# A two-block network on one Trainium2 core: full row tile in the feed-forward, mLSTM gates beside a value block, stabiliser spread by one stacked product

## The chip, the cores and the metric

The kernel runs as one launch on one core of one Trainium2 chip. The metric is the device time of an execution in microseconds (us). Before the change three runs took 2161.81, 2165.63 and 2168.8 us; the median is 2165.63 us.

## The reference: what is computed

A first block (two layers, 1024 channels, 16 + 256 positions) is followed by a second block (two layers, 256 latent and 256 context positions). In each layer of the first block a feed-forward stands before and another after the token mixer, four in all, with 2752 hidden channels:

```python
def swiglu_ffn(x, w13, w2):
    a, u = jnp.split(x @ w13, 2, axis=-1)
    return (jax.nn.silu(a) * u) @ w2
```

The first layer of the second block has two mixers side by side, neighbourhood attention (8 heads of 64) and a bidirectional mLSTM (4 heads of 128). Both read the same projection, whose last 16 columns are the mLSTM's gates: input and forget gate, per head and direction. In the chunked reference a stabiliser m keeps the exponentials in range:

```python
        d_in = jnp.where(lower, bcum[..., :, None] - bcum[..., None, :] + ic[..., None, :], -jnp.inf)
        m_inter = bcum + m_st[..., None]
        m_t = jnp.maximum(m_inter, jnp.max(d_in, axis=-1))
        w = jnp.exp(d_in - m_t[..., None])
```

The second layer's mixer is a latent attention; each layer ends with a convolutional feed-forward. Everything is float32.

## The kernel before, in words

**Products.** Activations lie with channels on partitions. A weight chunk (`chunk`, L130) is loaded by SP's queue into one of 4 raw buffers, ACT rounds it to fp32r (`whi`, L140) and DVE subtracts (`wlo`, L141); there are 5 buffers of each. `mm3` (L145) then makes a product of near float32 precision from three fp32r products: high weights with high and low activations (L147, L148), low weights with high activations (L149). Products in plain float32 are used for statistics, transposes and the attention.

**The feed-forward of the first block** (`ffn1`, L363). 43 column tiles of the gate/up product are swept; the first ten come from `raw_tiles`, in which the layer norm is applied to the product instead of the input, with POOL's help. `glu` turns a pair of tiles into a hidden tile and splits it into a tile of 128 partitions x 2 x 272. 2752 channels are 21 tiles of 128 and one of 64; that last one (c == 42) uses `ps[:64]` and `ps[64:128]` of one column tile, fills 64 partitions only, and is the 22nd and last hidden tile. The down-projection (from L398) makes 8 channel tiles; for each it goes over three weight chunks of 8, 8 and 6 row tiles, and over 22 row tiles in all; the last one uses 64 rows of weights and hidden tile (`hw`). DVE adds the residual (L408), ACT and DVE prepare the next norm, POOL sums. Beside the first block's feed-forwards `ada` (L331) computes the modulation vectors of the second block as DVE reductions.

**The first mixer of the second block** (`even`, L1221). `tiles` (L200) makes column tiles over 512 positions; its first `lead` tiles share a sweep over the inputs, first for the context half, then for the latent half, which becomes ready later, after the first block's last norm (PE's statistics `ps_x` and `ps_r`). The lead group here is the four query tiles and a tile with the 16 gate columns spread over 128 (`ev_wg`: forward input at 0, forward forget at 64, backward input at 32, backward forget at 96); the four key tiles follow one by one. `token_tiles` (L1232) makes products with tokens on partitions, two blocks of 256 columns by four token tiles, 24 products of 256 columns each; the attention's values are its first use. `ml_gates` (L1107) makes log forget gates, running sums and running maxima of the gates on ACT and DVE; `ml_cols` (L1138) transposes two of its results to columns. Then the attention runs, with the other mixer's products as filler. In `ml_weights` (L1156), per head, the stabiliser's row for a direction is spread over 128 partitions by a float32 product with a broadcast column of the identity (L1181); DVE masks it (L1183), ACT exponentiates pieces (L1195), DVE multiplies with the scores (L1196). Then two token products (`ps_tt`) serve as filler, and `ml_out` (L1203) applies the weights (`ps_mn`).

**Order.** Each engine runs its queue in order. The order in a queue is made when the program is built: instructions are taken by readiness and by the order in which the code gives them, with a few explicit priorities, and tiles get buffers in the same pass.

Of the kernel before, what the change touches and what calls it, by code (L numbers as in the profile page):

```python
# [11 lines left out]
F32 = mybir.dt.float32  # L12
F32R = mybir.dt.float32r
# [75 lines left out]
class Ker:  # L89
# [61 lines left out]
    def gemm(self, items, X, cols, mark=0, tail=0):  # L151
        """items: (PSUM tile, weight chunk) pairs that share the sweep over the rows of X, but for the last `tail` rows."""
        n = len(X)

        def step(ps, w, k):
            xh, xl = X[k]
            self.mm3(ps, w[0][:, k], w[1][:, k], xh[:, cols], xl[:, cols], k == 0, k == n - 1)

        for k in range(n - tail):
            if k == mark:  # L160
                self.mark = self.last
            for ps, w in items:
                step(ps, w, k)
        for ps, w in items:
            for k in range(n - tail, n):
                step(ps, w, k)

    def raw_tiles(self, srcs, ln, lead=2):
        """As tiles, of a layer norm's output, from its input scaled by the gain alone.

        Yields SBUF tiles that lack only the channel's bias, and the bias; the norm itself is made on the way."""
# [28 lines left out]
    def tiles(self, srcs, X, cols, kt=KD, lead=4, segs=None, hold=()):  # L200
        """Yields PSUM tiles of X @ w, one per 128-column chunk; the first `lead` share a sweep over X,
        one for each of segs, column ranges that become ready one after the other."""
        n = cols.stop - cols.start
        i = 0
        while i < len(srcs):
            g = lead if i == 0 else 1
            items = [((self.mm_ps if j < 4 else self.aux_ps)("ps_g")[:, :n],
                      self.chunk(s, kt, after=hold if 0 < i < lead + 2 else ()))
                     for j, s in enumerate(srcs[i:i + g])]
            if i == 0 and segs:  # L210
                for sl in segs:
                    part = [(ps[:, sl], w) for ps, w in items]
                    for a in ((part,) if sl is segs[0] else (part[:2], *([p] for p in part[2:]))):
                        self.gemm(a, X, sl)
            else:
                self.gemm(items, X, cols, tail=5 if g > 2 else 0)
            for ps, _ in items:
                yield ps
            i += g
# [6 lines left out]
    def mean_b(self, group, d, n, name, ps=None):  # L226
        """Mean over the channels of a group of tiles, the same in each partition."""
# [12 lines left out]
    def sqrt_table(self, after=None):  # L240
        """Have the square root's table in place before the chain that needs it."""
# [6 lines left out]
    def acc(self, S, key, m, src, n, eng):  # L248
        """Running sum over channel tiles; the eighth stays apart for the matmul that ends it."""
# [31 lines left out]
    def ln_raw(self, S, i, m, z, n):  # L281
        """Split of z times the gain of layer norm i, for raw_tiles."""
# [11 lines left out]
    def ln_start(self, S, i, eps, n, off, X):  # L294
        """Mean and reciprocal deviation, the same in each partition."""
# [5 lines left out]
    def ln_apply(self, S, i, eps, n, off, X, M, R, c):  # L301
        """State tile c <- its layer norm i; X gets the split of it."""
# [42 lines left out]
    def ada_cols(self, l):  # L345
        """Per-channel factors of layer l, [128, 8, 2] with the last axis (x, ctx)."""
# [16 lines left out]
    def ffn1(self, l, f, X, raw, n, off, ln):  # L363
        """SwiGLU; state <- 2 alpha state + ffn(state), and the sums of it."""
# [5 lines left out]
        def glu(pa, pu, hw):  # L370
# [5 lines left out]
            else:  # L376
                self.act = nc.scalar.activation(sa[:hw], pa, AF.Silu)
                self.dve = nc.vector.tensor_tensor(out=hr[:hw], in0=pu, in1=sa[:hw], op=ALU.mult)
            self.split(hr[:hw], ht[:hw, 0, :n], ht[:hw, 1, :n])
            hid.append((ht[:hw, 0, :n], ht[:hw, 1, :n]))  # L380
# [17 lines left out]
        for m in range(KD):  # L398
            ps = self.mm_ps("ps_y")[:, :n]
            for q in range(3):  # L400
                kt = 8 if q < 2 else 6
                wh, wl = self.chunk(self.A["w2"][i, m, q][:, :kt * 128], kt)
                for j in range(kt):
                    k = q * 8 + j
                    hw = 64 if k == KF1 - 1 else 128
                    self.mm3(ps, wh[:hw, j], wl[:hw, j], *hid[k], k == 0, k == KF1 - 1)
# [13 lines left out]
    def rope_ret(self, ps, dst):  # L420
        """dst <- ps * cos + halves swapped * signed sin, channels on partitions."""
# [11 lines left out]
    def conv_tap(self, l, u, y, t, j):  # L433
        """One tap of the causal depthwise convolution."""
# [65 lines left out]
    def ret_scores(self, h, q, k):  # L500
        """Decayed chunk-causal scores, keys on partitions."""
# [26 lines left out]
    def head_norm(self, tiles, eps):  # L528
        """Normalise each of the four 128-wide heads of token-major tiles (tile, rows)."""
# [182 lines left out]
    def tok_stats(self, groups, name, own=0, mm=False):  # L712
        """Mean over channels for each group, tokens on partitions: PSUM [128, 2] per group.

        The first `own` groups have a PSUM tile each, the others share one."""
# [18 lines left out]
    def tok_bcast(self, r, name):  # L734
        """r [128, nt] per token -> PSUM [128, 128 nt], the same in each partition."""
# [8 lines left out]
    def seg(self, c, s):  # L744
        """State columns of segment s (x, ctx)."""
# [7 lines left out]
    def mod_tile(self, x, R, mod, c, s):  # L753
        """Split of x * R * a + sh."""
# [9 lines left out]
    def first_mod(self, S, s):  # L764
        """The first modulated norm of a segment; S0 keeps the mean squares per token."""
# [11 lines left out]
    def res_sums(self, S, m, y, g, segs, more, w=None):  # L777
        """w = g * y, and the sums that both norms need. Returns w."""
# [21 lines left out]
    def acc2(self, S, key, m, src, segs, eng):  # L800
        """Running sums over channel tiles of the segments; the eighth stays apart."""
# [12 lines left out]
    def res_rows(self, S, s):  # L814
        """Factors of res_apply. The mean square of the new x follows from those of x, w and x * w."""
# [13 lines left out]
    def res_apply(self, ws, R, mod, s):  # L829
        """x += w * rstd(y), and the split of the modulated norm of the new x, for a segment."""  # L830
# [12 lines left out]
    def conv3(self, y, ps, w, b, n):  # L843
        """y = centred depthwise convolution of ps over each 256-token segment, plus bias."""
# [9 lines left out]
    def halves(self, items, product, finish, ws, S, mod):  # L854
        """The last channel tiles, first for x, whose norm then runs beside the products for ctx."""
# [39 lines left out]
    def ffn2(self, l, X, n, g, mod):  # L895
# [4 lines left out]
        for half in range(nh):  # L900
# [43 lines left out]
            def product1(m, ps, sl):  # L944
                """The same with each part of the weights loaded just before its use."""
# [38 lines left out]
    def to_tokens(self, a, c, dst):  # L984
        """Channel tile c to the token-major tiles dst[t][half]."""
# [4 lines left out]
    def out_start(self):  # L990
        """x with tokens on partitions, and room for the last residual."""
# [22 lines left out]
    def attention(self, jobs, nk, vs, group, outs, fill=iter(()), every=1):  # L1014
        """Softmax attention for jobs (scores, queries' output tile, value columns).

        jobs come `group` heads per output tile, the output tiles taking turns."""
# [52 lines left out]
    def to_channels(self, toks, c, n, dst, scale=None):  # L1070
        """Split of the c-th 128 channels of token-major tiles, transposed."""
# [35 lines left out]
    def ml_gates(self, ps):  # L1107
        """Rows at partitions 0..3 (forward heads) and 32..35 (backward heads)."""
# [28 lines left out]

    def ml_cols(self, c, B):  # L1138
        """The gates with keys on partitions: per key tile the stabiliser's part and the floor of the divisor."""
# [12 lines left out]
    # query columns that the keys of tile s reach: (forward, backward), diagonal block first  # L1152
# [3 lines left out]
    def ml_weights(self, h, q, k, M, cc):  # L1156
        """Stabilised gate weights times scores, keys on partitions, per direction and key tile."""
# [20 lines left out]
        for d in range(2):  # L1178
            r = 32 * d + h
            pm = self.aux_ps("ps_mb")  # L1180
            nc.tensor.matmul(pm, self.ident[:64, r:r + 1].to_broadcast([64, 128]), M, start=True, stop=True)  # L1181
# [39 lines left out]
    def even(self, X, g, mod):  # L1221
# [10 lines left out]
        def token_tiles(first, evac):  # L1232
            """Two 256-column blocks with tokens on partitions; yields after each product."""
            for c in range(2):
                w = [self.chunk(self.A["ev_tok"][first + c, i], 4, 256) for i in range(2)]
                for t in range(4):
                    ps = self.mm_ps("ps_tt")[:, :256]
                    ts = slice(t * 128, (t + 1) * 128)
                    mm = nc.tensor.matmul
                    for k, (xh, xl) in enumerate(X):  # L1240
                        wh, wl = w[k // 4][0][:, k % 4], w[k // 4][1][:, k % 4]
# [6 lines left out]
        it = self.tiles([A[c] for c in range(4)] + [self.A["ev_wg"]] + [A[c] for c in range(4, 8)], X, allc,  # L1248
                        lead=5, segs=(SEG[1][1], SEG[0][1]))
        first = [next(it) for _ in range(5)]  # L1250
        gates = first.pop()
        q = list(channel_tiles(first, lambda z, ps, i: nc.scalar.activation(z, ps, AF.Copy, scale=0.125)))
        k = list(channel_tiles(it, lambda z, ps, i: nc.scalar.copy(z, ps)))
        M, *cc = self.ml_gates(gates)
        va = [self.big("nav") for _ in range(4)]
        for _ in token_tiles(0, lambda t, c, ps: nc.scalar.copy(va[t][:, c * 256:(c + 1) * 256], ps)):
            pass
        cc = self.ml_cols(*cc)
        vb = [self.big("mlv") for _ in range(4)]
# [5 lines left out]
        def fill():  # L1265
            """Products for the other mixer, between the attention's."""
# [42 lines left out]
    def odd(self, X, g, mod):  # L1309
# [7 lines left out]
        def rms(groups):  # L1317
            """Splits of rms-normalised groups of (channel tile, gain, destination)."""
# [58 lines left out]
        def pair(j):  # L1377
            """Keys and queries of heads 2j and 2j + 1."""
# [73 lines left out]
def lay(I):  # L1452
# [80 lines left out]
    slots = (0, 64, 32, 96)  # L1533
    gb = np.zeros((128, 1), f)
    wg = np.zeros((D, 128), f)
    for i, p in enumerate(slots):
        gb[p:p + 4, 0] = I["ev_gate_b_2"][0, 4 * i:4 * i + 4]
        wg[:, p:p + 4] = I["ev_w_in_2"][0][:, 3584 + 4 * i:3588 + 4 * i]
    put("gate_b", gb)
    O["ev_wg"] = chunks(wg, [0], 128)[0]  # L1540
    ev = I["ev_w_in_2"][0]
    O["ev_in"] = chunks(ev, [128 * i for i in (*range(8), *range(12, 20))], 128)
    O["ev_tok"] = chunks(ev, [a + 256 * i for a in (1024, 2560, 3072) for i in range(2)], 256).reshape(6, 128, 2, 1024)
    O["ev_tok"] = np.ascontiguousarray(O["ev_tok"].transpose(0, 2, 1, 3))
# [70 lines left out]
```

## Time and profile before

| what | value |
|---|---|
| runs | 2161.81, 2165.63, 2168.8 us |
| span of the profiled execution, first to last instruction | 2156.3 us |
| own time of the profiled execution | not listed apart from its span; the median of the runs is 9.3 us above it |
| PE busy | 2088.8 us, 97% |
| DVE busy | 1575.5 us, 73% |
| ACT busy | 1097.3 us, 51% |
| POOL busy | 466.4 us, 22% |
| read from HBM | 324.92 MB, 151 GB/s over the span |

PE is the tensor engine's matmul side and PEld its weight loads; DVE, ACT, POOL and SP are the vector, scalar, GpSimd and sync engines. Matmuls are pipelined, so a matmul's duration overlaps its neighbours': what a product costs is read from the distance of starts. A group's row has its line, engine, operation, output and inputs, shape, count, busy time and mean; a timeline's row has start and duration in us, and in brackets the idle time of the engine before it and what ended it.

### The profile page before, as it was taken

What the parts mean: (1) busy time and instruction counts of PE and PEld (TensorE: products, weight loads), DVE (VectorE), ACT (ScalarE), POOL (GpSimd) and SP (SyncE); (2) the same over time, 40 slices, a digit from 0 to 9 for tenths busy, and PEclk for the clock granted to TensorE, in tenths of its full rate; (3) what the DMA queues carried; (4) which work ended last, traced back from release to release, by engine and by line L of the source; (5) the groups of instructions that cost most, each with busy time, mean ns of one, the idle gap of its engine ahead of it and who ended that gap; (6) DMA issues with size and microseconds to landing.
All of it is one profiled execution on the core that took longest, in us unless ns stands there. A gap on an engine that the chain in (4) does not pass through costs nothing.

```text
span 2156.3 us, 37011 instructions
## 1 busy us (share of the span) xinstructions
PE 2088.8 (97%) x14486; PEld 1920.0 (89%) x14486; DVE 1575.5 (73%) x2554; ACT 1097.3 (51%) x1870; POOL 466.4 (22%) x500
## 2 busy tenths in 40 slices
PE   7999889999999989999999999999999998999998
PEld 7999889999999978999988788888888888789998
DVE  8889898989897789887755546685435558568873
ACT  6444446544554445654546656554324455566663
POOL 5002795202500288600200000310000013211000
PEclk9999999999999999999999999999999999999999
DMA  8877334787587724587522211133243232024653
GB/s 275 271 238 270 100 121 160 245 268 242 175 283 252 253 99 130 159 290 252 186 91 91 69 50 36 44 99 87 76 121 93 69 103 87 22 78 137 185 178 109
DMA packets 96079, 328.38 MB, mean 152 GB/s; under 512 B 10912, under 2 KB 13600, under 8 KB 95648
## 3 DMA queue, kind: packets, MB, share of 16 engines
q1 hardware_dynamic: 95328, 325.45, 47.0%
q8 instruction: 114, 1.87, 0.3%
q10 hardware_dynamic: 576, 0.56, 0.1%
q14 instruction: 61, 0.50, 0.1%
HBM read 324.92 MB, written 1.05 MB: 151 GB/s over the span
## 4 chain that ended last, share of the span: by engine, by line
PE 82%; POOL 8%; DVE 6%; issue 3%; ACT 2%; DMA 0%; DVEq 0%; POOLq 0%; ACTq 0%
PE ps_g L147 14%; PE ps_g L148 13%; PE ps_g L149 13%; PE ps_y L147 4%; PE ps_y L148 4%; PE ps_y L149 4%; PE ps_d L149 3%; PE ps_d L147 3%; POOL cy L447 3%; PE ps_d L148 3%; POOL tap L446 2%; PE ps_o L1049 2%; PE ps_s L1414 1%; PE ps_r L147 1%; PE ps_r L149 1%
## 5 line engine op out<-in xcount | busy, mean ns | idle before, releaser
L140 ACT CAST whi<-raw 128x1024 fp32r<-128x1024 f32 (+2 forms) x527 | 535.2, 1017 | 607.7 <-issue 174.1
L141 DVE TENSOR_TENSOR wlo<-raw,whi 128x1024 fp32r<-128x1024 f32 (+2 forms) x527 | 633.9, 1212 | 250.8 <-ACT whi L140 247.6
L147 PE MATMUL ps_g<-xb,whi 128*128 128x272 f32 (+2 forms) x2320 | 707.1, 307 | 8.6 <-DVE rz L190 4.6
L148 PE MATMUL ps_g<-xb,whi 128*128 128x272 f32 (+2 forms) x2320 | 707.0, 305 | 2.8 <-DVE xb L315 1.9
L149 PE MATMUL ps_g<-xb,wlo 128*128 128x272 f32 (+2 forms) x2320 | 708.4, 306 | 1.3 <-DVE wlo L141 1.3
L147 PEld LDWEIGHTS ps_g<-xb,whi 128*128 128x128 f32 x2320 | 439.1, 190 | 28.0 <-ACT xb L314 3.7
L148 PEld LDWEIGHTS ps_g<-xb,whi 128*128 128x128 f32 x2320 | 440.8, 190 | 22.3 <-DVE xb L315 3.7
L149 PEld LDWEIGHTS ps_g<-xb,wlo 128*128 128x128 f32 x2320 | 439.6, 190 | 19.4 <-DVE wlo L141 1.5
L147 PE MATMUL ps_y<-hid,whi 128*128 128x272 f32 (+1 forms) x704 | 207.8, 295 | 0.0
L341 DVE SCALAR_TENSOR_TENSOR junk<-ada,silu_c 128x1024 bf16<-128x1024 f32 x160 | 201.6, 1260 | 0.0
L148 PE MATMUL ps_y<-hid,whi 128*128 128x272 f32 (+1 forms) x704 | 201.4, 286 | 0.0
L149 PE MATMUL ps_y<-hid,wlo 128*128 128x272 f32 (+1 forms) x704 | 200.9, 285 | 0.0
L147 PEld LDWEIGHTS ps_y<-hid,whi 128*128 128x128 f32 x704 | 132.4, 188 | 8.8 <-issue 0.8
L148 PEld LDWEIGHTS ps_y<-hid,whi 128*128 128x128 f32 x704 | 132.9, 189 | 0.0
L149 PEld LDWEIGHTS ps_y<-hid,wlo 128*128 128x128 f32 x704 | 132.3, 188 | 0.0
L147 PE MATMUL ps_r<-xb,whi 128*128 128x274 f32 (+1 forms) x384 | 112.7, 294 | 9.7 <-ACT whi L140 9.7
L149 PE MATMUL ps_r<-xb,wlo 128*128 128x274 f32 (+1 forms) x384 | 111.4, 291 | 2.7 <-DVE wlo L141 2.7
L148 PE MATMUL ps_r<-xb,whi 128*128 128x274 f32 (+1 forms) x384 | 111.7, 291 | 0.0
L254 POOL TENSOR_TENSOR acc_s<-st,st 128x272 f32<-128x272 f32 (+1 forms) x6 | 10.1, 1684 | 463.0 <-DVE st L408 433.0
L793 POOL TENSOR_TENSOR xw<-st,yd 128x512 f32<-128x512 f32 (+1 forms) x10 | 11.5, 1145 | 346.5 <-ACT yd L789 346.5
L147 PEld LDWEIGHTS ps_r<-xb,whi 128*128 128x128 f32 x384 | 73.2, 191 | 10.3 <-issue 9.8
L222 ACT CAST hid<-hr 128x272 fp32r<-128x272 f32 (+1 forms) x110 | 45.4, 412 | 64.4 <-DVE hr L375 33.0
(407 smaller groups left out, 3910.9 us busy)
## 6 DMA issues: line engine op xcount, KB each, us to landing
raw<-in_w SPq DMA_DIRECT2D x236, 512.0 KB, 4.7
ada<-in_ada SPq DMA_DIRECT2D x96, 512.0 KB, 4.3
raw<-in_wup SPq DMA_DIRECT2D x88, 512.0 KB, 3.5
raw<-in_w_in SPq DMA_DIRECT2D x44, 512.0 KB, 3.6
raw<-in_w SPq DMA_DIRECT2D x32, 384.0 KB, 3.9
raw<-in_wdn SPq DMA_DIRECT2D x24, 384.0 KB, 3.1
raw<-in_w_out SPq DMA_DIRECT2D x16, 512.0 KB, 3.6
raw<-in_ev_in SPq DMA_DIRECT2D x16, 512.0 KB, 3.5
```

The lines of the kernel that those rows point to most:

```text
L140: nc.scalar.copy(hi[:, :n], raw[:, :n])
L141: nc.vector.tensor_tensor(out=lo[:, :n], in0=raw[:, :n], in1=hi[:, :n].bitcast(F32), op=ALU.subtract)
L147: mm(ps, wh, xh, start=first, stop=False)
L148: mm(ps, wh, xl, start=False, stop=False)
L149: self.last = mm(ps, wl, xh, start=False, stop=last)
L222: self.nc.scalar.copy(hi, src)
L341: nc.vector.scalar_tensor_tensor(out=junk, in0=raw, scalar=1.0, in1=self.sc[:, s], op0=ALU.mult, op1=ALU.mult, accum_out=self.md[l][:, m, ...
L446: nc.gpsimd.tensor_scalar(out=p, in0=u[:, t, :L1 - s], scalar1=w, scalar2=0.0, op0=ALU.mult, op1=ALU.add)
L447: nc.gpsimd.tensor_tensor(out=y[:, t, s:], in0=y[:, t, s:], in1=p, op=ALU.add)
L793: nc.gpsimd.tensor_tensor(out=xw, in0=self.st[m][:, NM + sl.start:NM + sl.stop], in1=w[:, sl], op=ALU.mult)
L1049: nc.tensor.matmul(po[o][:, h * 64:(h + 1) * 64], pts[:, j * 128:(j + 1) * 128], vs(j, h), start=j == 0, stop=j == nj - 1)
L1414: nc.tensor.matmul(ps, qt[:96, h % 2, t * 128:(t + 1) * 128], kh[h % 2][:96], start=True, stop=True)
```

## The change

Three places.

**Full row tile.** In `glu` of the last hidden tile the other 64 partitions are cleared by a GpSimd memset, and the down-projection uses all 128 rows in its last row tile too. The weights' rows there were zero already.

```diff
+            if hw < 128:
+                nc.gpsimd.memset(ht[hw:].bitcast(F32), 0.0)
             self.split(hr[:hw], ht[:hw, 0, :n], ht[:hw, 1, :n])
-            hid.append((ht[:hw, 0, :n], ht[:hw, 1, :n]))
+            hid.append((ht[:, 0, :n], ht[:, 1, :n]))
...
-                    hw = 64 if k == KF1 - 1 else 128
-                    self.mm3(ps, wh[:hw, j], wl[:hw, j], *hid[k], k == 0, k == KF1 - 1)
+                    self.mm3(ps, wh[:, j], wl[:, j], *hid[k], k == 0, k == KF1 - 1)
```

**Gates as columns.** The gates' own column tile goes. Their 16 columns are appended to the first value block, which so has 272 columns and comes in three weight chunks of 3, 3 and 2 row tiles. DVE copies the 16 columns out for each token tile, PE transposes the four token tiles, and `ml_gates` starts from the transposed tile, after the first value block. The lead sweep now has the four query tiles and two of the four key tiles.

```diff
-                w = [self.chunk(self.A["ev_tok"][first + c, i], 4, 256) for i in range(2)]
+                if first + c == 0:
+                    cut, mc, src = (3, 3, 2), 272, self.A["ev_tokg"]
+                else:
+                    cut, mc, src = (4, 4), 256, self.A["ev_tok"][first + c - 1]
+                w, at = [], 0
+                for kt in cut:
+                    wh, wl = self.chunk(src[:, at * mc:(at + kt) * mc], kt, mc)
+                    w += [(wh[:, j], wl[:, j]) for j in range(kt)]
+                    at += kt
...
-        it = self.tiles([A[c] for c in range(4)] + [self.A["ev_wg"]] + [A[c] for c in range(4, 8)], X, allc,
-                        lead=5, segs=(SEG[1][1], SEG[0][1]))
-        first = [next(it) for _ in range(5)]
-        gates = first.pop()
+        it = self.tiles([A[c] for c in range(8)], X, allc, lead=6, segs=(SEG[1][1], SEG[0][1]))
+        first = [next(it) for _ in range(4)]
...
-        M, *cc = self.ml_gates(gates)
         va = [self.big("nav") for _ in range(4)]
-        for _ in token_tiles(0, lambda t, c, ps: nc.scalar.copy(va[t][:, c * 256:(c + 1) * 256], ps)):
-            pass
+        gt = self.big("gtok")[:, :512].rearrange("p (t g r) -> p t g r", g=4, r=32)
+        nc.gpsimd.memset(gt, 0.0)
+
+        def values(t, c, ps):
+            nc.scalar.copy(va[t][:, c * 256:(c + 1) * 256], ps[:, :256])
+            if c == 0:
+                nc.vector.tensor_copy(gt[:, t, :, :4], ps[:, 256:272].rearrange("p (g r) -> p g r", r=4))
+
+        for i, _ in enumerate(token_tiles(0, values)):
+            if i == 3:
+                pg = self.aux_ps("ps_tg")
+                for t in range(4):
+                    nc.tensor.transpose(pg[:, t * 128:(t + 1) * 128], gt[:, t].rearrange("p g r -> p (g r)"), self.ident)
+                M, *cc = self.ml_gates(pg)
         cc = self.ml_cols(*cc)
+        M = self.ml_stack(M)
```

**Stacked product.** The stabiliser's 64 rows are split into a rounded and a remaining part, which lie on partitions 0 to 63 and 64 to 127 of one fp32r tile; a selector matrix of two stacked identities picks a row and its remainder, so one fp32r product of 128 rows gives their sum on all partitions.

```diff
+    def ml_stack(self, M):
+
+        nc = self.nc
+        Ms = self.big("gms", F32R)[:, :512]
+        nc.scalar.copy(Ms[:64], M)
+        nc.vector.tensor_tensor(out=Ms[64:], in0=M, in1=Ms[:64].bitcast(F32), op=ALU.subtract)
+        pick = self.xp.tile([128, 64], F32R, name="pick")
+        nc.vector.tensor_tensor(out=pick, in0=self.ident[:, :64], in1=self.ident[:, 64:], op=ALU.add)
+        return Ms, pick
...
-            nc.tensor.matmul(pm, self.ident[:64, r:r + 1].to_broadcast([64, 128]), M, start=True, stop=True)
+            nc.tensor.matmul(pm, M[1][:, r:r + 1].to_broadcast([128, 128]), M[0], start=True, stop=True)
```

The layout on the host follows (the gate columns behind the first value block's, the gate bias at the same partitions as before). Comments and docstrings are emptied in place, so line numbers up to the new function stay.

## Rows read from the trace of the kernel before

**Rows 1.** The page, part 1: busy time and share of PE

```profile
PE 2088.8 (97%) x14486; PEld 1920.0 (89%) x14486; DVE 1575.5 (73%) x2554; ACT 1097.3 (51%) x1870; POOL 466.4 (22%) x500
```

**Rows 2.** The page, part 4: the chain that ended last, by engine

```profile
PE 82%; POOL 8%; DVE 6%; issue 3%; ACT 2%; DMA 0%; DVEq 0%; POOLq 0%; ACTq 0%
```

**Rows 3.** Stretches: us, busy PE PEld DVE ACT POOL (instructions), PEclk, DMA share, GB/s

```profile
60.00:148.50 88.50, 88.50 (x705) 88.50 (x704) 77.55 (x116) 39.16 (x58) 0.00 (x0) 1.00 0.80 268
...
157.30:200.00 42.70, 42.70 (x327) 41.49 (x327) 42.51 (x59) 18.55 (x25) 10.32 (x8) 1.00 0.75 247
...
235.00:277.00 42.00, 30.52 (x202) 27.45 (x203) 34.78 (x60) 18.11 (x32) 39.21 (x48) 0.92 0.29 88
...
1157.00:1237.00 80.00, 80.00 (x372) 57.16 (x372) 41.26 (x64) 52.39 (x77) 9.03 (x7) 1.00 0.26 83
```

**Rows 4.** Groups by line and form, whole span: the 64-row products

```profile
L147 PE MATMUL ps_y<-hid,whi 64*128 64x272 f32 x24 | 9.3, 388 | 0.0
```

**Rows 5.** Timeline, first down-projection: start, duration, engine, line, operands

```profile
154.04 0.29 PE L148 MATMUL ps_y<-hid,whi 128*128 128x272 f32 x1
...
156.17 0.19 PEld L148 LDWEIGHTS ps_y<-hid,whi 128*128 128x128 f32 x1
...
156.42 0.28 PE L149 MATMUL ps_y<-hid,wlo 128*128 128x272 f32 x1
...
156.63 0.39 PE L147 MATMUL ps_y<-hid,whi 64*128 64x272 f32 x1
...
156.86 0.29 PE L148 MATMUL ps_y<-hid,whi 64*128 64x272 f32 x1
...
157.44 0.29 PE L148 MATMUL ps_y<-hid,whi 128*128 128x272 f32 x1
```

**Rows 6.** Timeline of PE, fourth down-projection

```profile
1031.92 0.28 PE L149 MATMUL ps_y<-hid,wlo 128*128 128x256 f32 x1
...
1032.90 0.28 PE L148 MATMUL ps_y<-hid,whi 128*128 128x256 f32 x1
...
1034.67 0.61 PE L729 MATMUL ps_x<-mean,acc_x 128*128 128x1 f32 x4 [0.54 <-DVE acc_x L256]
```

**Rows 7.** Timeline of DVE, first down-projection

```profile
203.25 1.22 DVE L141 TENSOR_TENSOR wlo<-raw,whi 128x1024 fp32r<-128x1024 f32 x1
```

**Rows 8.** Timeline of PE, the same stage: first use of that split

```profile
209.72 0.29 PE L149 MATMUL ps_y<-hid,wlo 128*128 128x272 f32 x1
```

**Rows 9.** Timeline of DVE, gate chain: a memset

```profile
1135.78 0.48 DVE L1118 MEMSET on<- 64x512 f32 x1
```

**Rows 10.** Stretches, one tile's instructions: us, PE PEld DVE ACT / PE PEld ACT

```profile
1111.13:1133.45 22.32, 22.32 (x98) 17.88 (x96) 0.00 (x0) 1.75 (x3) 1.00 0.41 131
...
1133.45:1156.27 22.82, 22.82 (x192) 22.68 (x191) 2.59 (x7) 1.00 0.22 71
```

**Rows 11.** Timeline of PE, attention: four transposes

```profile
1168.77 0.60 PE L1038 MATMUL ps_pt<-ident,p 128*128 128x128 f32 x4
```

**Rows 12.** Timelines of ACT and DVE: first and last step of the gate chain

```profile
1134.85 0.68 ACT L1112 ACTIVATE gi<-ps_g,vec 64x512 f32<-64x512 f32 x1
...
1148.67 0.68 DVE L1135 TENSOR_TENSOR ge<-ge,gf 64x512 f32<-64x512 f32 x1
```

**Rows 13.** Timeline of all engines, second head of the mLSTM

```profile
1304.23 1.98 PE L1181 MATMUL ps_mb<-gf,ident 64*128 64x512 f32 x4
...
1306.14 0.39 PE L1242 MATMUL ps_tt<-whi,xb 128*128 128x256 f32 x1
...
1306.85 4.53 DVE L1196 TENSOR_TENSOR mw<-mw,ms 128x128 f32<-128x128 f32 x15
...
1311.93 4.63 PE L1210 MATMUL ps_mn<-mlv,mw 128*128 128x129 f32 x40
```

**Rows 14.** Timeline of all engines, first head

```profile
1290.11 1.28 ACT L1195 ACT_TABLE_LOAD   x1
...
1292.01 4.67 DVE L1196 TENSOR_TENSOR mw<-mw,ms 128x128 f32<-128x128 f32 x15
```

More of the change, by code (lines that the diff above doesn't have):

```diff
@@ L1234, in token_tiles @@
             for c in range(2):
-                w = [self.chunk(self.A["ev_tok"][first + c, i], 4, 256) for i in range(2)]
+                if first + c == 0:
[7 more added lines that the diff above has]
+                    at += kt
                 for t in range(4):
-                    ps = self.mm_ps("ps_tt")[:, :256]
+                    ps = self.mm_ps("ps_tt")[:, :mc]
                     ts = slice(t * 128, (t + 1) * 128)
@@ L1240, in token_tiles @@
                     for k, (xh, xl) in enumerate(X):
-                        wh, wl = w[k // 4][0][:, k % 4], w[k // 4][1][:, k % 4]
+                        wh, wl = w[k]
                         mm(ps, xh[:, ts], wh, start=k == 0, stop=False)
@@ L1532, in lay @@
     put("kv_g", cols(I["od_kv_norm_g_2"][0], 1))
-    slots = (0, 64, 32, 96)
+    ev = I["ev_w_in_2"][0]
     gb = np.zeros((128, 1), f)
-    wg = np.zeros((D, 128), f)
-    for i, p in enumerate(slots):
+    wg = []
+    for i, p in ((0, 0), (2, 32), (1, 64), (3, 96)):
         gb[p:p + 4, 0] = I["ev_gate_b_2"][0, 4 * i:4 * i + 4]
-        wg[:, p:p + 4] = I["ev_w_in_2"][0][:, 3584 + 4 * i:3588 + 4 * i]
+        wg.append(ev[:, 3584 + 4 * i:3588 + 4 * i])
     put("gate_b", gb)
-    O["ev_wg"] = chunks(wg, [0], 128)[0]
-    ev = I["ev_w_in_2"][0]
+    O["ev_tokg"] = chunks(np.concatenate([ev[:, 1024:1280]] + wg, axis=1), [0], 272)[0]
     O["ev_in"] = chunks(ev, [128 * i for i in (*range(8), *range(12, 20))], 128)
-    O["ev_tok"] = chunks(ev, [a + 256 * i for a in (1024, 2560, 3072) for i in range(2)], 256).reshape(6, 128, 2, 1024)
-    O["ev_tok"] = np.ascontiguousarray(O["ev_tok"].transpose(0, 2, 1, 3))
+    O["ev_tok"] = chunks(ev, [a + 256 * i for a in (1024, 2560, 3072) for i in range(2)][1:], 256)
     O["ev_out"] = chunks(I["ev_w_out_2"][0], [128 * i for i in range(8)], 128)
```

## The prediction

> **What bounds the kernel now.** I read the page first: PE is busy for 2088.8 of 2156.3 us [rows 1]. The chain that ended last says the same with the order of events in it: 82% PE, 8% POOL, 6% DVE [rows 2]. So a microsecond taken from PE counts, unless the stage is one where another engine paces it. The table by stretch tells which those are [rows 3]: in the gate/up sweep (60 to 148.5) and in the attention with its filler products (1157 to 1237) PE is never idle; in the convolution (235 to 277) PE has 30.5 of 42 us and POOL 39.2, a stretch that starts from PE's results and so moves as a whole; and in the first down-projection (157.3 to 200) PE is full, but DVE is too, with 42.51 of 42.70. That last row is the one to be careful with.
>
> **Part 1, the full row tile.** Each of the four feed-forwards of the first block has 8 down-projections of 22 row tiles; the last row tile has 64 rows, three products each, 96 in all; 24 of the 32 visits have 272 columns [rows 4], 8 have 256. Their own durations are like any other's. The cost is between them: full-row products start 0.1253 us apart (154.04 to 156.42 is 19 steps), but from the last full-row product (156.42) to the second one after the visit (157.44) are 1.02 us for 5 steps, where 0.63 would do: 0.39 us per visit, half of it on going in (156.42 to 156.63 to 156.86 are two steps of 0.22), half on coming out [rows 5]. With 256 columns it is the same: 1031.92 to 1032.90 is 0.98, five steps of 0.119, the pace of 256-column products in part 2, are 0.59: 0.39 [rows 6]. With 128 rows the visit becomes three more steps of the sweep. 32 x 0.39 = **12.5 us**, all in stretches where PE has no gap.
>
> What hides or takes back some of it. (a) In the first and the second feed-forward DVE is full, as its reductions for the modulation vectors stand between the weight splits. The weights' low part for the eighth channel tile is ready at 203.25 + 1.22 = 204.47 [rows 7], and PE uses it at 209.72 [rows 8]: 5.25 us of slack. PE will come 7 x 0.39 = 2.7 us sooner, DVE no sooner; 2.5 us are left, so PE doesn't wait. (b) In the fourth, PE stands at 1034.67 for DVE's sum of squares, 0.54 us [rows 6]; three visits stand ahead of it (1.2 us), of which the sum itself gains two (it starts after the second channel tile, 0.8 us). I take 0.4 us off. (c) The cleared half costs one GpSimd memset of 64 x 544 per feed-forward. No row has one; nearest are DVE's 64 x 512 at 0.48 us [rows 9] and, above, any POOL pass of 1 to 2 us. POOL has nothing in 60 to 148.5 [rows 3], the products that read the tile come 21 row tiles into the down-projection, and nothing is queued behind the memset there: nothing. Sum of part 1: **-12.1** (bounds -12.5 and -5.9, below).
>
> Rules against it: the weight load is 0.19 us long while products start 0.125 apart [rows 5], so full-row loads do run beside the product before. The Trainium skill, "TensorE: Matmul & The Clock Gate", section "The mechanism", has it that a load overlaps running matmuls only where its row group differs; by that the 96 products would expose their loads, 96 x 0.19 = 18.2 us more, and part 1 would come to +5.7. The rows speak against it: 21 of 22 row tiles have full rows now and keep the pace.
>
> **Part 2, gates as columns.** Removed: one channel tile of 24 products on both halves, 48 of 256 columns. At the pace of the value products, 22.82 / 192 = 0.1189 [rows 10], that is 5.71 us; its weight chunk (a DMA, a cast, a split) stood beside PE work. Added: two of the four key tiles now go in halves, 2 x (5.71 - 5.58) = 0.26, where 5.58 is a quarter of 22.32 us for the four full-width tiles (96 products; the 98 of the row count two that overlap its ends) [rows 10]. The lead sweep asks for six weight chunks and there are five buffers; the sixth is loaded when the first is done with, while PE has three more tiles for x (8.6 us) before it needs it: nothing. 96 products of the first value block grow from 256 to 272 columns: 96 x (0.1253 - 0.1189) = 0.61. Four transposes: four of the same size take 0.60 [rows 11]. Three chunks instead of two for that block, a gap-free strip of DVE copies and a memset lie beside. Net -5.71 + 0.26 + 0.61 + 0.60 = **-4.2** (bounds: -5.7 if the additions hide, 0 if a wait for the copies and for the stacked tile eats the rest).
>
> What moves is the gate chain. It began 1.4 us into the value products (1134.85, they begin at 1133.45) and its last DVE step ended at 1148.67 + 0.68 = 1149.35 [rows 12], 14.5 us later and 6.9 before the values ended. Now it begins after the first block and the transposes, 12.0 + 0.6 us in, and ends at 27.1, against 24.1 for the end of the values: it overhangs by 3 us into the attention. What it makes is needed only 130 us later, by the first head of the mLSTM. Queued behind it on ACT and DVE are the first heads' bias, maximum and exponential, but PE has the other mixer's products as filler there, whose chunks can be split while DVE waits for ACT's logarithm. I put it at nothing, with up to 6 us as the bound.
>
> **Part 3, the stacked product.** Per head two broadcast products of 64 rows in full float32: from 1304.23 to the next product at 1306.14 are 1.91 us [rows 13], eight products in all. In the rounded format a 512-column product takes 22.32 / 96 = 0.2325 [rows 10], and both halves of the number go in one stacked product: 0.47, and 0.5 with the way in. Saved at most 1.41 per head, 5.6 in all, if what follows is ready. After the filler (5.79 us, 1306.14 to 1311.93) PE needs the weights, which ACT and DVE make: DVE ends at 1306.85 + 4.53 = 1311.38, and that chain moves up by the shorter first product, two passes of 0.43 against one of 0.23, 0.6 us. PE arrives at 1310.5, the last weight it needs a little before 1310.8: 0.1 to 0.3 lost. In the first head ACT loads a table until 1290.11 + 1.28 = 1291.39 whatever PE does, and DVE's products then end at 1292.01 + 4.67 = 1296.68 [rows 14]; PE would arrive at 1295.7: half of the gain stays there. 3 x 1.3 + 0.7 = **-4.6** (bounds -5.6, and -2 if the chain doesn't move at all). Two extra conversions and the selector matrix are made 120 us ahead: nothing.
>
> **Sum.** -12.1 - 4.2 - 4.6 = -20.9 us, made against the profiled execution: span 2156.3, then 2135.4. The median of the runs, 2165.63, lies 9.3 above that span for what is outside of it; I keep these 9.3: **2144.7 us**. A measurement here tells 0.3%, some 6.5 us, from no change.
>
> **The rivals.**
> (1) DVE becomes the bound in the two feed-forwards where it is full: 16 visits x 0.39 = 6.2 us come back as waits for the low parts: 2150.9. For it: 42.51 of 42.70. Against: the slack of 5.25 us. Chance 0.12.
> (2) The late gate chain holds the attention: the 3 us that overhang, and as much again for the first jobs behind it: 2150.7. For it: in-order ACT and DVE. Against: the filler. Chance 0.12.
> (3) The change doesn't do what it says: the 0.39 us belongs to the last tile of an accumulation and not to its 64 rows, and stays: 2144.7 + 12.1 = 2156.8. For it: the 64-row visit is always the last of its accumulation. Against: half of it comes on entering, with two products of the same accumulation on both sides. Chance 0.04.
> (4) Slower: the memset stands in POOL's queue ahead of the normalisation's work at the head of the same sweep and waits there for the last hidden buffer, which the sweep reaches only at its end. POOL's scaling of the first ten tiles, and with it PE's PSUM buffers, then wait. For it: POOL takes its queue in order. It decides from (20.9 + 6.5) / 4 = 6.9 us per feed-forward; at 7 it gives 2144.7 + 28 = 2172.7. Against: that buffer is free when the sweep begins, and the split that writes its other half has the same wait now. Chance 0.03.
> (5) More than the sum: part 2's additions hide, as they are short, and part 3 keeps everything, if ACT's exponentials run ahead: -12.5 - 5.7 - 5.6 = -23.8, 2141.8. Chance 0.04.
> (6) The page's rule above: 2165.6 + 5.7 - 8.8 = 2162.5. Chance 0.01.
>
> **How the numbers follow.** The forecast has 0.64. Its own range takes in the bounds of parts 2 and 3 and three us for the median: 2139 to 2151; with (1), (2) and the measurement's spread on both sides it becomes 2137 to 2154. Faster by over 0.3% (below 2159.1): 0.64 + 0.12 + 0.12 + 0.04 and half of (3): 0.94; within 0.3%: the other half of (3), and (6): 0.03; slower: 0.03.
>
> **What would show it.** In the changed trace no product of the down-projection has 64 rows, and starts are 0.125 apart through the visits; the period of a channel tile falls from 8.64 to 8.25 us in all four feed-forwards (in the first two alone not: rival 1). From the end of x's norm to the first score of the attention PE is some 4 us shorter, with no gap at the transposes. PE goes on without a gap at the first scores (gaps: rival 2). A head of the mLSTM takes 13.5 instead of 14.83 us. I am wrong if the visits still cost 0.39, if POOL's memset has waiters, or if PE shows new gaps of over 5 us in all.

## The result, and the profile after

| | median, us (runs) | lowest to highest |
|---|---|---|
| before | 2163.72 (4) | 2161.26 to 2168.8 |
| after | 2145.82 (4) | 2143.17 to 2146.06 |

The ratio is 0.9917, 95% interval 0.9894 to 0.9941: some 17.9 us less (12.8 to 22.9). The forecast of 2144.7 us stands 1.1 below the median. Its parts don't stand as well as its sum: one of the three came out with the other sign.

The profiled execution of after took 2146.06 us, with a span of 2144.1. What lies outside of the span is 1.96 us, and between 1.7 and 2 in every other execution whose span is listed; the prediction took it for 9.3. The rest of the 9.3 is scatter: in a later series 22 executions of the kernel before had spans of 2153.8 (mean granted clock 0.986) to 2167.6 us (0.980), with 2159.3 in the middle, against 2156.3 in the profile. So the 12.2 us between the two profiled spans are less than the change gives; below, stages are compared with stages, and times by ratios.

The page of after, its busy times and its chain by engine (answering to [rows 1, 2]):

```profile
PE 2075.3 (97%) x14482; PEld 1920.3 (90%) x14482; DVE 1576.4 (74%) x2560; ACT 1096.5 (51%) x1871; POOL 472.3 (22%) x505
...
PE 85%; POOL 6%; DVE 5%; issue 2%; ACT 2%; DMA 0%; DVEq 0%; POOLq 0%; ACTq 0%
```

PE is still the bound. **The full row tile** shows in equal stretches of the third down-projection: how many products of `ps_y` go into 51.80 us. Before:

```profile
691.78:743.58 51.80, 51.80 (x398) 1.00 0.82 272
```

After (PE, PEld, DVE):

```profile
680.00:731.80 51.80, 51.80 (x416) 51.80 (x415) 2.62 (x6) 1.00 0.86 278
```

416 against 398 is 4.5% more; the period of a channel tile fell from 8.63 to 8.27 us, where the prediction has 8.64 and 8.25. No product of `ps_y` has 64 rows any more, and in the first three down-projections none starts more than 0.13 us after the one before ([rows 5] had steps of 0.21 to 0.23). The clearing is one short pass on POOL per feed-forward, 94 us ahead of the down-projection, with nobody waiting (timeline of POOL, after):

```profile
54.06 0.55 POOL L380 MEMSET hid<- 64x544 f32 x1
```

**The gates' columns.** The stretches that answer to [rows 10], after (one tile's instructions each; PE PEld DVE ACT):

```profile
1078.91:1115.57 36.66, 34.30 (x240) 31.82 (x240) 0.00 (x0) 3.99 (x7) 1.00 0.29 91
...
1115.57:1127.62 12.05, 12.05 (x96) 11.98 (x95) 0.53 (x3) 1.12 (x3) 1.00 0.15 45
```

The queries and keys got shorter, the 272-column block is at 12.05 / 96 = 0.1255 us a product, as expected. But then PE stands. Its waits from 1100 to 1300 us, after:

```profile
PE ps_gt L1155 <- DVE ge L1136: 3.4, 1, 3.4
PE ps_gt L1155 <- DVE gi L1133: 1.0, 1, 1.0
```

The timeline of PE at that place, after:

```profile
1139.50 0.28 PE L1263 MATMUL ps_tt<-whi,xb 128*128 128x256 f32 x1
1140.78 0.27 PE L1155 MATMUL ps_gt<-ident,gi 64*128 64x64 f32 x1 [1.00 <-DVE gi L1133]
1144.46 0.37 PE L1155 MATMUL ps_gt<-ident,ge 64*128 64x64 f32 x1 [3.41 <-DVE ge L1136]
...
1145.26 2.02 PE L1101 MATMUL ps_s<-ez 64*128 64x512 f32 x2
1147.21 0.79 PE L147 MATMUL ps_qk<-xb,whi 128*128 128x512 f32 x1
...
1150.36 0.63 PE L148 MATMUL ps_qk<-xb,whi 128*128 128x512 f32 x1
1150.79 0.50 PE L149 MATMUL ps_qk<-xb,wlo 128*128 128x512 f32 x1
1151.13 0.40 PE L147 MATMUL ps_qk<-xb,whi 128*128 128x512 f32 x1
1151.36 0.40 PE L148 MATMUL ps_qk<-xb,whi 128*128 128x512 f32 x1
```

`ps_gt` are the transposes of `ml_cols`. The first waits for `gi`, the second for `ge`, the gate chain's last result, and behind them in PE's queue stands `ps_s`, the attention's first score. The chain, after: its first step on ACT, its first and last on DVE, and DVE's first work for the attention's softmax:

```profile
1129.89 0.69 ACT L1113 ACTIVATE gi<-ps_tg,vec 64x512 f32<-64x512 f32 x1 [0.55 <-PE ps_tg L1284]
...
1136.35 0.68 DVE L1118 SCALAR_TENSOR_TENSOR gf<-gf,ge 64x512 f32<-64x512 f32 x1 [5.22 <-ACT ge L1117]
...
1143.72 0.68 DVE L1136 TENSOR_TENSOR ge<-ge,gf 64x512 f32<-64x512 f32 x1
...
1147.70 0.42 DVE L1104 TENSOR_TENSOR ps_s<-ps_s,nab 128x256 f32<-128x256 f32 x1
```

The chain takes 14.5 us, as before (1129.89 to 1144.40), but it begins 14.3 us into the values, where the prediction had 12.6.

And once PE goes on, products start 0.43 us apart instead of 0.23. The window of the profile says why:

```profile
1144.20:1151.00 6.80, 6.54 (x18) 4.27 (x19) 4.58 (x7) 2.58 (x5) 0.00 (x0) 0.50 0.56 166
```

The granted clock is 0.50 there, the lower level (1.2 GHz); PE had been idle for 4.41 us but for one transpose. The two scores take 1.95 us to the next start instead of 1.00, the 12 products behind them 4.71 instead of 2.97: 2.7 us on top of the wait.

**The stacked product**, second head, PE, after (answering to [rows 13]):

```profile
1292.72 1.03 PE L1182 MATMUL ps_mx<-ez 128*128 128x256 f32 x4
1293.40 0.81 PE L1192 MATMUL ps_mb<-gms,pick 128*128 128x512 f32 x2
...
1294.05 0.28 PE L1261 MATMUL ps_tt<-whi,xb 128*128 128x256 f32 x1
...
1299.73 0.72 PE L1221 MATMUL ps_mn<-mlv,mw 128*128 128x129 f32 x5
```

The broadcasts take 0.65 us to the next start (1.91 before), `ps_mx` ahead of them 0.68 (0.96 before), the filler 5.68 (5.79), and `ps_mn` starts without a wait. From head to head are 13.19 us, before 14.83.

### The profile page after: what moved, and what is told of

It is laid out like the page before. It is cut to its first block, busy times and chain, and to the rows that moved or that the text cites. A ratio compares the mean times of both kernels' runs of the same rounds, so it can differ in the third digit from the quotient of the medians.

```text
span 2144.1 us, 37020 instructions
## 1 busy us (share of the span) xinstructions
PE 2075.3 (97%) x14482; PEld 1920.3 (90%) x14482; DVE 1576.4 (74%) x2560; ACT 1096.5 (51%) x1871; POOL 472.3 (22%) x505
## 4 chain that ended last, share of the span: by engine, by line
PE 85%; POOL 6%; DVE 5%; issue 2%; ACT 2%; DMA 0%; DVEq 0%; POOLq 0%; ACTq 0%
PE ps_g L147 14%; PE ps_g L149 14%; PE ps_g L148 14%; PE ps_y L148 4%; PE ps_y L149 4%; PE ps_y L147 4%; PE ps_d L149 3%; PE ps_d L148 3%; PE ps_d L147 3%; PE ps_o L1050 2%; POOL cy L448 1%; PE ps_s L1443 1%; PE ps_s L1101 1%; PE ps_r L149 1%; PE ps_r L148 1%
## 5 line engine op out<-in xcount | busy, mean ns | idle before, releaser
L148 PE MATMUL ps_y<-hid,whi 128*128 128x272 f32 (+1 forms) x704 | 202.2, 287 | 0.0
L147 PE MATMUL ps_y<-hid,whi 128*128 128x272 f32 (+1 forms) x704 | 202.2, 287 | 0.0
```

The source lines that it names most:

```text
L147: mm(ps, wh, xh, start=first, stop=False)
L148: mm(ps, wh, xl, start=False, stop=False)
```

## The experiments

Each of the first three makes one part of the change alone, so that the sum can be checked term by term.

### Part 1 alone

Edit: the kernel before with the first of the three diffs.

> The full row tile alone. Theory (tile-shape switches cost 0.39 us per visit and go): no 64-row product in the four down-projections, their eight channel tiles 8 x 0.39 = 3.1 us shorter each except the fourth, where PE waits for the sum of squares and then runs for a while at half clock; 11 to 12.5 us faster than before in all. Rival (the 0.39 us belongs to the last tile of an accumulation): the visits keep 1.02 us and the time stays within 2 us of before. Rival (DVE takes the first two back): 5 to 7 us faster.

Measured: median 2148.36 us (6 runs), the kernel before on the same chip 2161.07 (22); ratio 0.9926 (0.9904 to 0.9949), 16.0 us less (11 to 21). From the first to the last product, the four down-projections take 65.80, 65.98, 65.98 and 66.71 us, to the hundredth as in after, against 69.25, 68.73, 68.73 and 67.52. The first three gain 3.45, 2.75 and 2.75; the prediction has 3.1 for each. The fourth gains 0.8 only: PE waits 1.15 us for the squares instead of 0.54, and later runs at the lower clock for some 3 us. Together that is 9.8 us, and the way out of each last visit, 0.2 us, stands behind the last product: 10.5. Why the medians differ by 5 us more, no stage shows.

### Part 2 alone

Edit: the kernel before with the second diff, but for its `ml_stack` line, which belongs to part 3.

> The gates as columns of the value block alone. Theory (PE waits at the transposes of the gate columns, which stand in its queue ahead of the attention's first score, 3.9 us, and some 2.7 us are lost to half clock behind it): first score of the attention not earlier than before relative to the end of x's norm by more than 1 us, and the time 0 to 3 us slower than before. Rival (the net of products removed and added, as predicted, with no wait): 4.2 us faster.

Measured: median 2165.28 us (12 runs), ratio 1.0016 (1.0005 to 1.0028): 3.5 us **more**. PE's waits around the attention's start, this kernel:

```profile
PE ps_gt L1144 <- DVE ge L1135: 3.4, 1, 3.4
...
PE ps_gt L1144 <- DVE gi L1132: 1.0, 1, 1.0
```

The waits of after, without the other two parts. The part that was to give 4.2 us takes 3.5 (1 to 6).

### Part 3 alone

Edit: the kernel before with the third diff.

> The stacked fp32r product alone. Theory (per head 14.83 to 13.2 us, as the products get shorter by 1.26 us and the two tile-shape switches at their ends go, 0.38 us): 6.5 us faster than before. Rival (the weights' chain on ACT and DVE holds the next products, as predicted): 4.6 us faster, with gaps of PE ahead of the first product with the weights.

Measured: median 2154.78 us (11 runs), ratio 0.9970 (0.9957 to 0.9982), 6.5 us less (4 to 9). The distance between heads is 13.19 us, as in after.

The three parts sum up to -16.0 + 3.5 - 6.5 = -19.0 us; together they gave -17.9. Within the intervals nothing is left over, so each can be judged by itself.

### The same change, the transposes later

Edit to the kernel after: the transposes of the gate columns stand between the two attentions, not ahead of both.

```diff
-        cc = self.ml_cols(*cc)
         M = self.ml_stack(M)
...
+        cc = self.ml_cols(*cc)
```

> The changed kernel with the transposes of the gate columns, and what follows them, given after the first attention. Theory (what costs is the place of these transposes in PE's queue, not the lateness of the gate chain): no gap of PE at the first scores, full clock there, and 5 to 7 us faster than the changed kernel, some 23 to 25 faster than before. Rival (the late chain itself, on ACT and DVE, holds the attention's first jobs): the first scores' weights still come late, a gap of 3 us or more moves behind the first jobs, and the time stays within 2 us of the changed kernel.

Measured: median 2137.38 us (6 runs), ratio to the kernel before 0.9891 (0.9871 to 0.9911), some 23.6 us less than before. Against the kernel after, of another series, the time alone decides nothing, as the intervals overlap (0.9894 to 0.9941 there); the stretches below do. The first score now follows the value products at the full clock (PE, this kernel), but a part of the gain is given back 20 us later:

```profile
1138.30 0.28 PE L1263 MATMUL ps_tt<-whi,xb 128*128 128x256 f32 x1
1138.51 1.12 PE L1101 MATMUL ps_s<-ez 64*128 64x512 f32 x2
...
1158.41 1.10 PE L1050 MATMUL ps_o<-nav,pts 128*128 128x64 f32 x8 [1.30 <-ACT pts L1044]
```

### Part 2 alone, the transposes later

Edit: as above, to the kernel before with the second diff. It asks whether the sum of part 2 was right and only the transposes' place wrong.

> The kernel before with part 2 alone, and the gate columns' transposes between the two attentions. Theory (the sum of part 2, -4.2 us, was right, and all that went wrong is that PE's queue had the transposes that wait for the gate chain ahead of the first scores): from the statistics of x's norm to the first score of the attention 63 us instead of 66.7 before and 67.9 with part 2 alone, at the full clock; time some 4 us below the kernel before, ratio 0.998. Rival (2) in its own form (the gate chain's ACT and DVE work delays the attention's exponentials wherever the transposes stand): PE waits of 3 us or more in the first 30 us of the attention, and a ratio of 1.000 or above.

Measured: median 2160.62 us (12 runs), ratio 0.9996 (0.9986 to 1.0006): no change that can be told from none. Each theory had a half. From the statistics to the first score are 62.33 us, as the first one said (63); but PE has a new wait in the attention and the lower clock behind it, as rival (2) said, though of 2.43 us and not of 3 or more. The way from the gate chain to that wait, timelines of all engines, this kernel:

```profile
1151.44 0.69 PE L1100 MATMUL ps_s<-ez 64*128 64x512 f32 x1
...
1155.45 0.68 DVE L1135 TENSOR_TENSOR ge<-ge,gf 64x512 f32<-64x512 f32 x1
...
1157.20 0.42 DVE L1103 TENSOR_TENSOR ps_s<-ps_s,nab 128x256 f32<-128x256 f32 x1
1157.53 1.21 DVE L141 TENSOR_TENSOR wlo<-raw,whi 128x1024 fp32r<-128x1024 f32 x1
...
1158.77 0.33 SPq L134 DMA_DIRECT2D raw<-in_ev_tok  x1
1159.15 0.42 SPq L1094 DMA_DIRECT2D nab<-in_rpb  x1
...
1164.99 1.28 POOL L1096 TENSOR_TENSOR nab<-nab,namask 128x512 f32<-128x512 f32 x1 [65.63 <-DMA nab<-in_rpb]
1166.30 0.43 DVE L1103 TENSOR_TENSOR ps_s<-ps_s,nab 128x256 f32<-128x256 f32 x1 [2.22 <-POOL nab L1096]
...
1167.46 1.28 ACT L1295 ACT_TABLE_LOAD   x1 [4.62 <-DVE ez L851]
...
1171.37 0.57 ACT L1043 COPY pts<-ps_pt 128x512 f32<-128x512 f32 x1
...
1172.00 1.10 PE L1049 MATMUL ps_o<-nav,pts 128*128 128x64 f32 x8 [2.43 <-ACT pts L1043]
```

The first score starts at 1151.44, but its bias is added at 1157.20, behind the gate chain's last step (1155.45): 5.8 us, where the kernel before had 2.0 (1156.83 to 1158.87). The weight splits stand behind the chain as well. The last of them ends at 1158.74, and 0.03 us later SP, whose next chunk had to wait for that raw buffer, goes on; behind the chunk in its queue is the bias of the next head (`nab`), which POOL has at 1164.99. DVE adds it at 1166.30, the other mixer's work on DVE and ACT comes behind, and `pts`, which `ps_o` needs, at 1171.37. In the kernel before that bias is added at 1167.58, 10.8 us after the first score; here 14.9 after it. So the scores came 4.4 us sooner and the softmax behind them stayed where it was. To load the bias ahead of the chunks wasn't tried, so this way is read from the trace and not shown by a run.

So the account of part 2 runs over three stretches of PE: from the statistics of x's norm to the first value product, from there to the attention's first score, and on to the mLSTM's first score (`ps_ms`). In us, from the starts in PE's timelines:

| kernel | to the values | to the scores | to the mLSTM | sum |
|---|---|---|---|---|
| before | 43.32 | 23.37 | 128.37 | 195.07 |
| part 2 alone | 38.22 | 29.70 | 131.09 | 199.01 |
| part 2, transposes later | 38.20 | 24.14 | 132.73 | 195.07 |
| after | 36.66 | 29.69 | 131.06 | 197.41 |
| after, transposes later | 36.66 | 24.14 | 132.07 | 192.87 |
| the same, in the last experiment below | 36.67 | 24.14 | 130.37 | 191.17 |

The first three rows have the same mean clock of 0.96 in the first stretch, the others 1.00, which is worth 1.5 us. The removal gives 5.1 us in the first stretch. In the second the additions cost 24.14 - (23.37 - 0.56) = 1.3, where 0.56 are the eight `ps_gt` that no longer stand there. Together -3.8, where the prediction had -4.2. The wait at the transposes adds the rest of the second stretch, 29.70 - 23.37 - 1.3 = 5.0: 4.4 of waiting, and the transposes at the lower clock. In the third stretch the lower clock takes 2.7. Together +3.9, beside 3.5 measured. With the transposes later both go, but 2 to 4.4 come back in the third stretch: 0.55 for the transposes themselves, 1.1 to 2.4 for the wait of `ps_o`, 0.4 for a wait of `ps_qk` in the last two rows, and some 1.5 where the lower clock followed (not in the last row).

### The order of the row tiles

Edit to the kernel before: every second channel tile takes its row tiles in another order, the 64-row one first.

```diff
+            order = list(range(KF1))
+            if m % 2:
+                order = [KF1 - 1, *range(16, KF1 - 1), *range(16)]
...
-                    self.mm3(ps, wh[:hw, j], wl[:hw, j], *hid[k], k == 0, k == KF1 - 1)
+                self.mm3(ps, wh[:hw, j], wl[:hw, j], *hid[k], x == 0, x == KF1 - 1)
```

> The kernel before, with the row tiles of every second channel tile taken in another order, so that its 64-row tile comes first, right behind the 64-row tile of the channel tile before it. All 96 products of 64 rows stay; the changes between 64 and 128 rows are halved. Theory (the 0.39 us of a visit is paid at the two changes of row count): two visits side by side cost 0.39 together, 4 feed-forwards x 4 pairs x 0.39 = 6.2 us come back, the ratio is about 0.997, and the odd channel tiles end on full rows without a delay. Rival (3) (it belongs to the last tile of an accumulation): the odd channel tiles show 0.39 at their end on full rows, a 64-row tile at the head of an accumulation costs nothing, and the time is that of before. A third possibility (each 64-row product costs 0.13 by itself): the pair costs 0.78, the time is that of before.

Measured: median 2157.07 us (8 runs), ratio 0.9966 (0.9952 to 0.9979), 7.3 us less (4.5 to 10.4), where 6.2 were expected. In 51.80 us of the third down-projection 406 products, halfway between 398 and 416. PE there, this kernel:

```profile
686.70 0.28 PE L149 MATMUL ps_y<-hid,wlo 128*128 128x272 f32 x1
686.91 0.39 PE L147 MATMUL ps_y<-hid,whi 64*128 64x272 f32 x1
687.14 0.28 PE L148 MATMUL ps_y<-hid,whi 64*128 64x272 f32 x1
687.27 0.29 PE L149 MATMUL ps_y<-hid,wlo 64*128 64x272 f32 x1
...
687.52 0.28 PE L148 MATMUL ps_y<-hid,whi 64*128 64x272 f32 x1
687.64 0.28 PE L149 MATMUL ps_y<-hid,wlo 64*128 64x272 f32 x1
687.86 0.39 PE L147 MATMUL ps_y<-hid,whi 128*128 128x272 f32 x1
688.09 0.30 PE L148 MATMUL ps_y<-hid,whi 128*128 128x272 f32 x1
```

Six products of 64 rows, one end of an accumulation and one beginning, and between them steps of 0.125: the slow steps, two on going in and two on coming out, are at the changes of row count alone. Rival (3) is out, and so is a price per product. The Trainium skill, "TensorEngine Tiling (Array Packing)", section "Key Properties", says that a change of the tiling mode drains the engine. If 64 rows count as another mode, the trace agrees, with 0.2 us for each change.

### Float32 over 128 rows

Edit to the kernel before: the stabiliser's rows lie in a cleared tile of 128 partitions, and the float32 broadcast goes over all of them.

```diff
-            nc.tensor.matmul(pm, self.ident[:64, r:r + 1].to_broadcast([64, 128]), M, start=True, stop=True)
+            nc.tensor.matmul(pm, self.ident[:, r:r + 1].to_broadcast([128, 128]), M, start=True, stop=True)
```

> The kernel before with the stabiliser's broadcast product still in float32, but over 128 rows: the 64 rows below are cleared, the selector is a column of the whole identity. It tells the share of the row count from that of the number format. Theory (the change of row count costs on entering and leaving, as in the feed-forward): the stretch of the product ahead (ps_mx) falls from 0.96 to 0.68 us and the filler's from 5.79 to 5.68 as with the stacked product, the two broadcasts stay near 1.8, and a head falls from 14.83 to about 14.4 us. Rival (all of it is the format): no stretch changes and a head stays at 14.8.

Measured (one execution, so by its trace alone): from head to head 14.44 us, as expected to a few hundredths. PE, second head, this kernel:

```profile
1312.04 1.03 PE L1178 MATMUL ps_mx<-ez 128*128 128x256 f32 x4
1312.90 1.88 PE L1188 MATMUL ps_mb<-gms,ident 128*128 128x512 f32 x4
1314.22 0.68 PE L1249 MATMUL ps_tt<-whi,xb 128*128 128x256 f32 x1
...
1320.30 0.38 PE L1217 MATMUL ps_mn<-mlv,mw 128*128 128x129 f32 x2
```

The saving is not shared out as I had said: `ps_mx` has 0.86, the broadcasts 1.32 and the filler 6.08; why, is not shown. The sum of the three stretches tells: 8.66 before, 8.26 here, 7.01 after. Of the 1.65 us per head, 0.40 go with the two changes of row count and 1.25 with the format.

### The squares later

Edit to the kernel after with the transposes later: in the fourth feed-forward the statistics of the context's norm were to stand one channel tile later.

> The kernel after, with the gate columns' transposes between the two attentions, and in the fourth feed-forward the statistics of the context's norm one channel tile later (behind the third channel tile, the squares stay behind the second). Theory: the wait of 1.15 us at that statistic goes, and with it the 3.4 us at the lower clock behind it, where 14 products took 3.11 us instead of 1.67: 2.5 us less than with the gate columns moved alone, some 26 us below the kernel before (ratio 0.988). Rival: the clock falls there without the wait too, or the squares come late at any place as DVE is full with weight splits: less than 1 us (ratio 0.989 or above).

Measured: median 2138.63 us (5 runs), ratio 0.9894 (0.9877 to 0.9911). The edit moved nothing; PE, this kernel:

```profile
1023.71 0.61 PE L734 MATMUL ps_x<-mean,acc_x 128*128 128x1 f32 x4 [1.15 <-DVE acc_x L256]
```

That is the place and the wait of after (1023.77, 1.15 us): these products already stood behind the third channel tile. So it is a second measurement of the order with the transposes later, and the two agree (0.9891, 0.9894). It also takes down my account of the lower clock at that place: the wait is the same in both kernels, but here, as in the first kernel with the transposes later, the clock stays up, and the fourth down-projection takes 65.18 instead of 66.71 us. The reverse is there too: with part 2 or part 3 alone it drops (69.06 instead of 67.52 us), though neither touches that stage. What lets it drop there stays open.

## Why the prediction was right, and where not

**Part 1: right in its mechanism.** 0.39 us per visit, at the two changes of row count; -12.1 predicted, -16.0 measured with an interval of 11 to 21, of which the stages show 10.5. "PE doesn't wait" in the first two feed-forwards held, and rival (1) didn't come. The wait for the fourth's squares grew by 0.6 instead of 0.4, and no term had the lower clock in that stage. The memset cost nothing, so rival (4) is out. Rival (6) is out too: the 96 products now have full rows, and go at the pace of the others, without a step above 0.13 us, beside loads of 0.19 us. It came from the Trainium skill, "TensorE: Matmul & The Clock Gate", section "The mechanism"; the prediction took its sentence on row groups alone, while the section also lets a load that targets the background weight buffer go ahead of running products, and with that the trace agrees.

**Part 2: the wrong sign.** The terms were good (-3.8 for -4.2). What failed is the step "I put it at nothing", and the reason for it, "What it makes is needed only 130 us later, by the first head of the mLSTM". The trace of before says otherwise, in two lines of PE that the prediction leaves out:

```profile
1156.27 0.27 PE L1144 MATMUL ps_gt<-ident,gi 64*128 64x64 f32 x1
...
1156.83 1.07 PE L1100 MATMUL ps_s<-ez 64*128 64x512 f32 x2
```

The last consumer is 130 us away, but the first one, the transpose to columns, stands on PE directly ahead of the attention's first score. The chain ended 6.9 us ahead of it before the change, and 4.6 after the last value product now, where the prediction had 3. I had asked what is queued behind the chain on ACT and DVE, and not what the chain's own products stand in front of on PE. Rival (2) is what happened, at about its price: "up to 6 us", measured 5.0 for the wait at the transposes, and 2.7 more for the clock behind it, which no term had. The form it was given, in-order ACT and DVE holding the attention, is there too, and came to light when the wait on PE was taken away.

**Part 3: right, undersized.** -4.6 predicted, -6.5 measured, 6.6 in the four heads by the trace, beyond the part's own bound of 5.6; 13.5 us per head predicted, 13.19 measured. Two terms were off. The gain was counted from the start of the broadcast, and 0.28 of it lies ahead of that, in the stretch of `ps_mx` (0.96 from the line below to the broadcast's start in [rows 13], 0.68 after):

```profile
1303.27 1.03 PE L1171 MATMUL ps_mx<-ez 128*128 128x256 f32 x4
```

And "0.1 to 0.3 lost" to the weights did not come: `ps_mn` starts with DVE still at work, since its 40 products need the weights one after the other. For the same reason the first head, put at 0.7, gave 1.66 like the others: with part 3 alone DVE ends at 1292.75 + 4.84 = 1297.59, over a microsecond after `ps_mn` began at 1296.34.

**The base.** -20.9 was set against a span that stood some 3 us below the middle of later executions, and 9.3 us were called outside of the span, of which 1.9 are. As I only carried the difference over to the median, this did no harm. Of the sum, +7.7 in part 2 was paid for by -3.9 in part 1 and -1.9 in part 3; that the total came within 3 us is partly luck. The stages say so more plainly: -10.5 in the down-projections, +2.3 from the statistics to the mLSTM (195.07 to 197.41) and -6.6 in its four heads make -14.8, 6 us short of -20.9, and still within the interval of what was measured.

**The signs.** From the statistics to the first score PE was to be 4 us shorter; it is 0.35 (66.70 to 66.35). And "new gaps of over 5 us in all", the prediction's own sign of being wrong, is just reached: 4.41 us at the transposes and 0.61 more at the squares.

## What to carry to other kernels

When a chain of work moves later, look up the first instruction that reads it, on every engine, and what stands behind that instruction in its queue; when the last result is needed says nothing. A change of row count between neighbouring products costs PE 0.2 us each way here, so a short tile is cheaper padded, or at least put next to another short one. And a wait of PE may be paid again in the granted clock behind it: 4.4 us of waiting cost 2.7 more here, while behind the wait of 1.15 us the clock fell in some kernels and not in others.

## What was not expected of the hardware

- The lower clock after the wait at `ps_gt`: 6.8 us at 0.50, in both kernels with the transposes early, for 2.7 us on top of 4.4 us of waiting.
- The scatter of executions of one kernel goes with the mean granted clock: spans of 2153.8 us at 0.986 and 2167.6 at 0.980 for the kernel before; 2133.8 at 0.986 and 2142.7 at 0.981 for the last one above. What differs between two profiles by less than that has to be looked for in one stage, not in the span.
